# The first three projection units get their own order and one norm for all tokens

## The chip, the cores and the metric

The kernel runs on one core of a Trainium2 chip. The metric is the device time of one execution in microseconds (us), less is better. Where one profiled execution is read, times are from its first instruction.

## The reference

One step of a two-layer streaming encoder over 1056 tokens (1024 new frames and 32 frames of a running stream), model width 1024, all in float32. What the change touches is the entrance of layer 0:

```python
def _rmsnorm(x, g):
    xf = x.astype(jnp.float32)
    y = xf * lax.rsqrt(jnp.mean(xf * xf, axis=-1, keepdims=True) + EPS)
    return (y * g.astype(jnp.float32)).astype(x.dtype)

def _mixer_a(h, ctx, w_in, conv_w, w_out):
    gb, gc, u = jnp.split(h @ w_in, 3, axis=-1)
    z, new_ctx = _causal_dwconv(gc * u, ctx, conv_w)
    return (gb * z) @ w_out, new_ctx
```

`h` is `_rmsnorm(x, a_norm)`. Behind it come a gated feed-forward net with a width-3 convolution, a combined key/value projection, forgetting attention over 16 heads, and a second feed-forward net. The outputs are the normed stream, the new keys, values and forget logits, and the convolutions' last rows.

## The kernel before

Everything is held transposed: a tile is 128 features by 1056 tokens, and `x` is eight such tiles (`NK` = 8). A float32 product is made of three matmuls in a rounded format: each operand is split into a high part (ScalarE, `AF.Copy` into float32r) and a low part (VectorE, the rest), and `chain` adds high*high, high*low and low*high into one PSUM bank for each of the eight feature blocks.

A *unit* (`unit`) is one weight tile of 1024 by 128 against all tokens: three chunks `CH` of 352 tokens, 8 blocks, 3 matmuls, so 72 matmuls. `w_in` has 24 units. The mixer (`mixer`, its `make(t)`) takes them in threes: `gc` (unit `NK+t`), `u` (`2*NK+t`), then `gb` (`t`); gc times u, a convolution, times gb. The first three units here are gc, u and gb of t = 0, the fourth to sixth those of t = 1.

The row norm is applied after the product: it is one factor per token. `normed` splits each x tile (with the gain folded in), squares it on ScalarE and adds the squares (`square_add`: GpSimd, for the last tile VectorE) into `acc`. While the factor is not known, the first two units run with the blocks outermost (`outer`), as x tiles come in, and are evicted raw. Then `settle` calls `rstd`, chunk by chunk: four matmuls sum the squares of 4 x 88 tokens over the features (L334), ScalarE takes the square root, VectorE the reciprocal with a correction step, a diagonal tile `dg` is built, and one matmul with ones spreads the factor over all 128 rows (L348). `settle` multiplies the raw gc and u; units from the third on multiply on eviction (L294).

The loads stand on SP's queue in program order: gains, x0's first third, the first unit's weights in two pieces (blocks 0 to 1, then 2 to 7), the rest of x. The weight staging tile `wraw` has one buffer, so a unit's weights are asked for when the one before has been split; split weights (`wh`, `wl`) share four buffers. The order of the work on each engine is set by the tile framework's scheduler, which follows a timeline of its own, except inside `strict()`, where instructions of TensorE, VectorE and ScalarE keep their program order (all such instructions bear the line of the wrapper, L73). PSUM has eight banks' worth of tiles: three `d`, two double `s`, one `o`; `dbank` goes round d, d, d, s, s, o.

## Time and profile before

| | us |
|---|---|
| median of 3 runs | 2549.89 (2549.51 to 2549.95) |
| the profiled execution | 2550.09 |
| its span, first to last instruction | 2548.3 |
| mean granted TensorE clock | 0.989 |
| TensorE busy | 2471.9 (97%) |
| start of the fourth unit on TensorE | 64.67 |

In the rows of the profile PE is TensorE's matmuls, PEld its weight loads, DVE VectorE, ACT ScalarE, POOL GpSimd and SP the queue that issues the loads. A row names the line, the operation, output<-input and the shape; "xN" counts instructions merged into a row, whose duration is then that of all. A bracket holds the idle time before an instruction and what ended it. In tables by stretch the granted clock stands behind the engines' busy times, 1.00 being full speed.

### The profile page before, as it was taken

How to read it: one execution, taken by the hardware profiler on the slowest of the kernel's cores; microseconds unless marked ns; L12 is line 12 of the kernel's file. 1: busy time of each engine (PE TensorE's matmuls, PEld its weight loads, DVE VectorE, ACT ScalarE, POOL GpSimd, SP SyncE). 2: the span in 40 equal slices, each digit the busy share in tenths (PEclk: the TensorE clock that was granted, in tenths of full speed). 3: DMA queues.
4: the chain of work that ended last, by engine and by line, in shares of the span. 5: the costliest groups of instructions: out<-in, count | busy, mean ns of one | idle time of the engine just before them, and what ended most of it. 6: DMA issues, size and time to landing. Idle time of an engine off the chain costs nothing. (4 is left out here: it accounts for less than half of the span.)

```text
span 2548.3 us, 47227 instructions
## 1 busy us (share of the span) xinstructions
PE 2471.9 (97%) x18484; PEld 2433.1 (95%) x18484; DVE 1531.6 (60%) x2617; ACT 1216.5 (48%) x2388; POOL 899.3 (35%) x952
## 2 busy tenths in 40 slices
PE   7999999999999999998999999999999999999996
PEld 6999999999999999997999999999999999999996
DVE  5434438855555555665677677665875555555575
ACT  4111114555555555444566666653454555555454
POOL 3000012344444444342455444422244444443423
PEclk9999999999999999998999999999999999999998
DMA  3111123376766666631233222373247676666752
GB/s 111 45 48 50 42 77 98 70 120 120 122 119 114 116 118 119 139 113 50 75 80 80 77 76 71 80 251 104 72 88 125 116 121 119 111 117 116 122 141 69
DMA packets 147631, 254.76 MB, mean 100 GB/s; under 512 B 22352, under 2 KB 58320, under 8 KB 147408
## 3 DMA queue, kind: packets, MB, share of 16 engines
q0 software_dynamic: 41472, 77.88, 23.0%
q1 hardware_dynamic: 105936, 173.87, 22.7%
q8 instruction: 145, 2.38, 0.4%
q14 instruction: 78, 0.64, 0.1%
HBM read 130.52 MB, written 113.04 MB: 96 GB/s over the span
## 5 line engine op out<-in xcount | busy, mean ns | idle before, releaser
L711 PE MATMUL pb_p<-b,wb 128*128 128x264 f32 x6720 | 894.9, 284 | 1.8 <-ACT u L753 1.8
L711 PEld LDWEIGHTS pb_p<-b,wb 128*128 128x128 f32 x6720 | 850.0, 188 | 2.2 <-ACT u L753 2.2
L877 POOL DMA_DIRECT2D xd<-xs x288 | 262.1, 914 | 494.9 <-ACT xs L875 493.6
L875 ACT ACTIVATE xs<-pb_d 128x264 f32<-128x264 f32 x576 | 218.3, 387 | 349.4 <-PE pb_d L261 309.8
L259 PE MATMUL pb_d<-acth,wb 128*128 128x264 f32 x1152 | 327.8, 285 | 1.6 <-ACT xs L875 1.6
L260 PE MATMUL pb_d<-actl,wb 128*128 128x264 f32 x1152 | 327.5, 285 | 0.0
L261 PE MATMUL pb_d<-acth,wb 128*128 128x264 f32 x1152 | 327.3, 285 | 0.0
L259 PE MATMUL pb_d<-xh,wh 128*128 128x384 f32 (+2 forms) x864 | 285.3, 333 | 8.4 <-ACT xh L248 7.6
L260 PE MATMUL pb_d<-xl,wh 128*128 128x384 f32 (+2 forms) x864 | 285.2, 330 | 5.6 <-DVE xl L249 5.5
L261 PE MATMUL pb_d<-xh,wl 128*128 128x384 f32 (+2 forms) x864 | 283.6, 328 | 0.0
L478 DVE SCALAR_TENSOR_TENSOR y<-u,cv,y 128x1058 f32<-128x1058 f32 x186 | 238.8, 1329 | 54.9 <-ACT y L474 54.8
L259 PEld LDWEIGHTS pb_d<-acth,wb 128*128 128x128 f32 x1152 | 216.6, 188 | 2.8 <-ACT xs L875 2.5
L261 PEld LDWEIGHTS pb_d<-acth,wb 128*128 128x128 f32 x1152 | 216.8, 188 | 0.0
L260 PEld LDWEIGHTS pb_d<-actl,wb 128*128 128x128 f32 x1152 | 216.8, 188 | 0.0
L236 ACT ACTIVATE wh<-wraw 128x1024 fp32r<-128x1024 f32 (+1 forms) x69 | 72.3, 1047 | 259.6 <-PE pb_o L260 125.3
L460 POOL COPY u<-cv 128x4 f32<-128x4 f32 x96 | 63.5, 662 | 355.7 <-DVE u L668 256.9
L701 DVE TENSOR_TENSOR wb<-wr,wb 128x512 fp32r<-128x512 f32 x196 | 154.2, 788 | 56.0 <-ACT wb L700 44.7
L701 DVE TENSOR_TENSOR wb<-ws,wb 128x512 fp32r<-128x512 f32 x160 | 126.1, 789 | 98.6 <-ACT wb L700 98.6
L259 PEld LDWEIGHTS pb_d<-xh,wh 128*128 128x128 f32 x864 | 164.7, 191 | 9.8 <-ACT xh L248 8.0
L260 PEld LDWEIGHTS pb_d<-xl,wh 128*128 128x128 f32 x864 | 165.1, 191 | 7.9 <-DVE xl L249 7.4
L733 POOL TENSOR_TENSOR ws<-wr 128x512 f32<-128x512 f32 x80 | 121.7, 1521 | 134.9 <-DMA wr<-in_w_up 120.8
L261 PEld LDWEIGHTS pb_d<-xh,wl 128*128 128x128 f32 x864 | 164.8, 191 | 0.3
(347 smaller groups left out, 4964.2 us busy)
## 6 DMA issues: line engine op xcount, KB each, us to landing
xd<-xs POOLq DMA_DIRECT2D x288, 264.0 KB, 4.3
wr<-in_w_up SPq DMA_DIRECT2D x168, 256.0 KB
wr<-in_w_down SPq DMA_DIRECT2D x80, 256.0 KB
x<-xd SPq DMA_DIRECT2D x48, 264.0 KB
wraw<-in_w_in SPq DMA_DIRECT2D x23, 512.0 KB
xd<-x SPq DMA_DIRECT2D x64, 132.0 KB
wraw<-in_w_kq SPq DMA_DIRECT2D x16, 512.0 KB
xd<-x SPq DMA_DIRECT2D x16, 264.0 KB
```

The source lines that it names most:

```text
L236: nc.scalar.activation(h[:, i:j], raw[:, i:j], AF.Copy)
L259: nc.tensor.matmul(ps, wh, xh[:, c[0]:c[1]], start=(i == 0), stop=False)
L260: nc.tensor.matmul(ps, wh, xl[:, c[0]:c[1]], start=False, stop=False)
L261: nc.tensor.matmul(ps, wl, xh[:, c[0]:c[1]], start=False, stop=(i == n - 1))
L460: self.nc.gpsimd.tensor_copy(v, st.rearrange("p (a b) -> p a b", b=2))
L478: self.nc.vector.scalar_tensor_tensor(y, u[:, i:i + TC], w[:, i:i + 1], y, op0=OP.mult, op1=OP.add)
L701: nc.vector.tensor_sub(t[:, 1], src, t[:, 0].bitcast(F32))
L711: nc.tensor.matmul(ps[:, q, :QB], w[:, i, k], t[:, j, cs], start=(begin and k == 0 and n == 0), stop=(end and k == len(b) - 1 and n == 2), ...
L733: getattr(self.nc.gpsimd, "tensor_" + op)(dst, x, y)
L875: nc.scalar.activation(t[:, q * QB:(q + 1) * QB], ps, AF.Copy)
L877: nc.gpsimd.dma_start(d, t, accum_op=OP.add)
```

## The change

The first three units move into a function of their own, `opening`, which runs under `strict()`, so that its written order is the engines' order:

- Loads: each of the three weight tiles has its own staging slot, and the second unit's weights are asked for before x4, the third's after x7.
- High and low parts of all x tiles come first; the weights' blocks 2 to 7 of unit 1 are split after x1. The squares of x follow on ScalarE while unit 2 runs, and VectorE adds all of them. GpSimd does nothing here.
- A one-column square root at the start has ScalarE load the table with Sqrt before any other work.
- The third unit starts before the norm is known. Between its first and second chunk twelve matmuls sum the squares of all 1056 tokens; between its second and third three matmuls spread the factor. gc, u and gb are then all scaled by VectorE, chunk by chunk.
- Each product block runs chunk by chunk with its three matmuls together.

`mixer` takes the finished gc, u and gb for t = 0. From the fourth unit on, the order on each engine is the same as before, but for two matmuls of the attention that change places.

ScalarE at the start of the program, before and after (x_99 is x0, x_100 is x1 and so on; wr is the new staging slot, nrm the tile of the small norm steps):

```order
L236 ACTIVATE wh<-wraw 128x256
L236 ACTIVATE wh<-wraw 128x768
L248 ACTIVATE xh<-x_99,gain 128x352 x3
L307 ACTIVATE acc<-x_99 128x1056
L248 ACTIVATE xh<-x_100,gain 128x1056
L310 ACTIVATE sq<-x_100 128x1056
L248 ACTIVATE xh<-x_101,gain 128x1056
L310 ACTIVATE sq<-x_101 128x1056
```

```order
L73 ACT_TABLE_LOAD
L73 ACTIVATE nrm<-epst 88x1
L73 ACTIVATE wh<-wr 128x256
L73 ACTIVATE xh<-x_99,gain 128x352 x3
L73 ACTIVATE xh<-x_100,gain 128x1056
L73 ACTIVATE wh<-wr 128x768
L73 ACTIVATE xh<-x_101,gain 128x1056
```

The larger weight piece went behind x1, and the squares left the row of high parts; they stand behind the split of the second unit's weights now.

VectorE behind the last low part, before and after (x_106 is x7; the lines L237 are weight splits of later units):

```order
L249 SCALAR_TENSOR_TENSOR xl<-x_106,gain,xh 128x1056
L311 TENSOR_TENSOR acc<-acc,sq 128x1056
L237 TENSOR_TENSOR wl<-wraw,wh 128x1024 x2
L338 TENSOR_SCALAR nw<-pb_d 88x4
L339 RECIPROCAL nr<-ne 88x4
```

```order
L73 SCALAR_TENSOR_TENSOR xl<-x_106,gain,xh 128x1056
L73 TENSOR_TENSOR wl<-wr,wh 128x1024
L73 TENSOR_TENSOR sq<-sq 128x1056
L237 TENSOR_TENSOR wl<-wraw,wh 128x1024
L73 TENSOR_TENSOR sq<-sq 128x1056 x3
L73 TENSOR_TENSOR wl<-wr,wh 128x1024
L73 TENSOR_TENSOR sq<-sq 128x1056 x3
L237 TENSOR_TENSOR wl<-wraw,wh 128x1024
L73 TENSOR_SCALAR nrm<-pb_s 88x12
```

VectorE now does all seven adds and four weight splits between the last low part and the norm, and the norm's small steps come once, for 12 columns.

TensorE between the end of unit 2 and the third unit, before (a piece without gaps) and after (the rows of the norm alone, each standing behind 24 matmuls of the third unit's first and second chunk):

```order
L261 MATMUL pb_o<-xh,wl 128x352
L334 MATMUL pb_d<-ones,acc 88x1 x4
L348 MATMUL pb_d<-dg,ones 128x352
L334 MATMUL pb_d<-ones,acc 88x1 x4
L259 MATMUL pb_d<-xh,wh 128x352
```

```order
L73 MATMUL pb_d<-xh,wl 128x352
L73 MATMUL pb_s<-ones,sq 88x1 x12
L73 MATMUL pb_d<-xh,wh 128x352
...
L73 MATMUL pb_d<-xh,wl 128x352
L73 MATMUL pb_s<-dg,ones 128x352
L73 MATMUL pb_o<-dg,ones 128x352
```

The sums had stood between unit 2 and the third unit with nothing between them and the first broadcast; now a chunk of 24 matmuls stands ahead of each. The diff:

```diff
@@ -654,23 +654,146 @@
         self.nc.sync.dma_start(cw, taps)
         return st, cw, out
 
-    def mixer(self, x, parts, after):
+    def opening(self, x, gain):
+
+
+        nc, a = self.nc, self.a
+        ACT, DVE, PE = nc.scalar, nc.vector, nc.tensor
+        srcs = [a["w_in"][i].rearrange("p (k c) -> p k c", c=128) for i in (NK, 2 * NK, 0)]
+        raw = [self.slot("wr", [128, NK, 128]) for _ in srcs]
+        w = [[self.wp.tile([128, NK, 128], F32R, name=n, tag="w") for n in ("wh", "wl")] for _ in range(2)]
+        w.append([self.slot(n, [128, NK, 128], F32R) for n in ("wh", "wl")])
+        xs = [[self.keep("x" + i, dt=F32R) for i in "hl"] for _ in range(NK)]
+
+        def load(m, c=(0, TT)):
+            nc.sync.dma_start(x[m][:, slice(*c)], a["x"][m][:, slice(*c)])
+
+        def fetch(u, i=0, j=NK):
+            nc.sync.dma_start(raw[u][:, i:j], srcs[u][:, i:j])
+
+        def whigh(u, i=0, j=NK):
+            ACT.activation(w[u][0][:, i:j], raw[u][:, i:j], AF.Copy)
+
+        def wlow(u, i=0, j=NK):
+            DVE.tensor_sub(w[u][1][:, i:j], raw[u][:, i:j], w[u][0][:, i:j].bitcast(F32))
+
+        def high(m, c=(0, TT)):
+            ACT.activation(xs[m][0][:, slice(*c)], x[m][:, slice(*c)], AF.Copy, scale=self.gain[:, gain, m:m + 1])
+
+        def low(m, c=(0, TT)):
+            cs = slice(*c)
+            DVE.scalar_tensor_tensor(xs[m][1][:, cs], x[m][:, cs], self.gain[:, gain, m:m + 1],
+                                     xs[m][0][:, cs].bitcast(F32), op0=OP.mult, op1=OP.subtract)
+
+        def products(u, ks):
+            ws = [(w[u][0][:, k], w[u][1][:, k]) for k in range(NK)]
+            for t, c in zip(banks[u], CH):
+                self.chain(t, ws, xs, c, ks)
+
+        def evict(u, i):
+            for p, d in spread(CH[i], before[u]):
+                ACT.activation(out[u][:, d], banks[u][i][:, p.start - CH[i][0]:p.stop - CH[i][0]], AF.Copy)
+
+        load(0, CH[0])
+        fetch(0, 0, 2)
+        fetch(0, 2, NK)
+        for c in CH[1:]:
+            load(0, c)
+        for m in range(1, NK):
+            load(m)
+            if m in (3, 7):
+                fetch(m // 4 + 1)
+        before = (0, PAD, 0)
+        out = [self.slot("gc"), self.slot("u", [128, TC + PAD]), self.slot("gb")]
+        banks = [[self.dbank()[:, :c[1] - c[0]] for c in CH] for _ in range(2)]
+        warm = self.slot("nrm")[:SIDE, :3 * TT // SIDE].rearrange("p (i n) -> p i n", i=3)
+        e, v, r = (warm[:, i] for i in range(3))
+        ACT.activation(e[:, :1], self.epst[:SIDE], AF.Sqrt)
+        whigh(0, 0, 2)
+        high(0, CH[0])
+        wlow(0, 0, 2)
+        low(0, CH[0])
+        for c in CH[1:]:
+            high(0, c)
+            low(0, c)
+        products(0, range(1))
+        for m in range(1, NK):
+            high(m)
+            low(m)
+            if m == 1:
+                whigh(0, 2)
+                wlow(0, 2)
+            products(0, range(m, m + 1))
+        whigh(1)
+        wlow(1)
+        sq = [self.slot("sq") for _ in range(NK)]
+        for m in range(NK):
+            ACT.activation(sq[m], x[m], AF.Square)
+            if m:
+                DVE.tensor_add(sq[0], sq[0], sq[m])
+            products(1, range(m, m + 1))
+            if m == 1:
+                for i in range(3):
+                    evict(0, i)
+            if m == 4:
+                whigh(2)
+                wlow(2)
+        banks.append([self.dbank()[:, :c[1] - c[0]] for c in CH])
+        evict(1, 0)
+        ws = [(w[2][0][:, k], w[2][1][:, k]) for k in range(NK)]
+        self.chain(banks[2][0], ws, xs, CH[0])
+        n = TT // SIDE
+        ps = self.bank("s")[:SIDE, :n]
+        for i in range(n):
+            PE.matmul(ps[:, i:i + 1], sq[0][:, i * SIDE:(i + 1) * SIDE], self.ones[:, :1], start=True, stop=True)
+        ACT.activation(e, ps, AF.Sqrt, bias=self.epst[:SIDE], scale=1.0 / D)
+        DVE.tensor_scalar(v, ps, -0.5 / D, -0.5 * EPS, op0=OP.mult, op1=OP.add)
+        DVE.reciprocal(r, e)
+        DVE.tensor_mul(e, r, r)
+        DVE.tensor_mul(e, e, v)
+        DVE.scalar_tensor_tensor(r, e, 1.5, r, op0=OP.add, op1=OP.mult)
+        evict(1, 1)
+        evict(1, 2)
+        self.rs = self.slot("rstd")
+        dg = self.slot("dg")[:SIDE, :TT].rearrange("p (n c) -> p n c", c=SIDE)
+        self.chain(banks[2][1], ws, xs, CH[1])
+        for i, c in enumerate(CH):
+            b = slice(c[0] // SIDE, c[1] // SIDE)
+            shape = [SIDE, b.stop - b.start, SIDE]
+            DVE.tensor_mul(dg[:, b], self.ident[:SIDE, None, :SIDE].to_broadcast(shape),
+                           r[:, b, None].to_broadcast(shape))
+            ps = self.bank("sos"[i])[:, :c[1] - c[0]]
+            PE.matmul(ps, self.ones[:SIDE], dg[:, b].rearrange("p n c -> p (n c)"), start=True, stop=True)
+            ACT.activation(self.rs[:, slice(*c)], ps, AF.Copy)
+        for i, c in enumerate(CH):
+            if i == 2:
+                self.chain(banks[2][i], ws, xs, c)
+            for u in range(2):
+                for p, d in spread(c, before[u]):
+                    DVE.tensor_mul(out[u][:, d], out[u][:, d], self.rs[:, p])
+            DVE.tensor_mul(out[2][:, slice(*c)], banks[2][i], self.rs[:, slice(*c)])
+        return xs, out
+
+    def mixer(self, x, xs, opened, after):
         a, nc = self.a, self.nc
-        xs = [parts[k] for k in range(NK)]
         st, cw, out = self.convs(a["st_a"], a["cw_a"], NK)
 
         def make(t):
-            gc = self.slot("gc")
-            self.unit(a["w_in"][NK + t], xs, gc)
-            u = self.slot("u", [128, TC + PAD])
-            self.unit(a["w_in"][2 * NK + t], xs, u, PAD)
+            if t == 0:
+                gc, u, gb = opened
+            else:
+                gc = self.slot("gc")
+                self.unit(a["w_in"][NK + t], xs, gc)
+                u = self.slot("u", [128, TC + PAD])
+                self.unit(a["w_in"][2 * NK + t], xs, u, PAD)
             for p, d in spread((0, TT), PAD):
                 nc.vector.tensor_mul(u[:, d], u[:, d], gc[:, p])
             self.halo(u, st[:, t])
             self.tail(out[:, t], u)
             y = self.conv(u, cw[:, t])
-            gb = self.slot("gb")
-            self.unit(a["w_in"][t], xs, gb)
+            if t:
+                gb = self.slot("gb")
+                self.unit(a["w_in"][t], xs, gb)
             for p, d in spread((0, TT), PAD, PAD):
                 nc.vector.tensor_mul(y[:, d], y[:, d], gb[:, p])
             return self.split(y, "act", keep=False, cuts=spread((0, TT), PAD, PAD))
@@ -1351,19 +1474,11 @@
     nc = net.nc
     net.consts()
     x = [net.keep(f"x{m}") for m in range(NK)]
-    for m in range(NK):
-        for c in CH if m == 0 else ((0, TT),):
-            nc.sync.dma_start(x[m][:, c[0]:c[1]], a["x"][m][:, c[0]:c[1]])
-            if m == 0 and c == CH[0]:
-                net.ready.append(net.weights(a["w_in"][NK], cuts=((0, 2), (2, 8))))
-        if m == 1:
-            net.ready.append(net.weights(a["w_in"][2 * NK]))
     with net.phase(SLOTS):
-        f, acc, parts = net.normed(x, "x", 0, True)
-        for m in range(NK):
-            f(m)
-        net.start(acc, 2)
-        net.mixer(x, parts, net.normalise(x, 1))
+        net.fresh = 0
+        with net.strict():
+            opened = net.opening(x, 0)
+        net.mixer(x, *opened, net.normalise(x, 1))
     with net.phase(UPSLOTS, banks=UPBANKS):
         f, acc, parts = net.normed(x, "x", None)
```

## The prediction

> **What bounds the kernel now.** I read the page first, to see which engine sets the time.
>
> ```profile
> span 2548.3 us, 47227 instructions
> PE 2471.9 (97%) x18484; PEld 2433.1 (95%) x18484; DVE 1531.6 (60%) x2617; ACT 1216.5 (48%) x2388; POOL 899.3 (35%) x952
> ```
>
> TensorE is busy 97% of the span, so what the change can win is TensorE's idle and slow time in the stage it touches. The busy times by stretch, cut at the events of that stage, come second. Columns: stretch, length, busy time of PE, PEld, DVE, ACT, POOL with counts, granted clock, DMA share, GB/s.
>
> ```profile
> 7.64:13.00 5.36, 5.25 (x15) 4.17 (x16) 3.43 (x6) 5.30 (x7) 1.18 (x1) 1.00 0.99 398
> 13.00:23.50 10.50, 5.72 (x32) 4.84 (x31) 10.50 (x4) 10.50 (x11) 10.26 (x4) 1.00 0.45 177
> 43.70:46.37 2.67, 0.00 (x0) 0.03 (x1) 2.04 (x7) 1.10 (x2) 0.00 (x0) 0.52 0.25 57
> 48.78:53.90 5.12, 5.12 (x18) 5.12 (x19) 1.75 (x8) 0.26 (x1) 0.00 (x0) 0.50 0.01 2
> 53.90:64.67 10.77, 10.77 (x69) 10.30 (x69) 3.19 (x12) 1.19 (x3) 0.00 (x0) 0.99 0.01 2
> 64.67:76.21 11.54, 11.54 (x74) 11.54 (x73) 9.81 (x14) 3.43 (x4) 1.31 (x2) 1.00 0.16 45
> 76.00:300.00 224.00, 224.00 (x1399) 224.00 (x1398) 92.69 (x135) 36.53 (x39) 9.15 (x14) 1.00 0.15 45
> ```
>
> The last two rows are the yardstick. From 64.67 us TensorE never rests for 235 us, and a unit of 72 matmuls takes 11.54 us (0.16 each). The three units before that end at 64.67 us although they hold 34.6 us of matmuls: 30 us are lost. So the question is one: when does the fourth unit start after the change? Whatever that start gains, 235 us of unbroken TensorE work behind it carry on.
>
> The timeline, by engine, shows who is waited for in the first two units (start, duration, instruction, what ended the idle time).
>
> ```profile
> 4.48 0.42 ACT L236 ACTIVATE wh<-wraw 128x256 fp32r<-128x256 f32 x1 [2.46 <-DMA wraw<-in_w_in]
> 6.27 0.84 ACT L236 ACTIVATE wh<-wraw 128x768 fp32r<-128x768 f32 x1 [1.37 <-DMA wraw<-in_w_in]
> 7.02 1.53 ACT L248 ACTIVATE xh<-x,gain 128x352 fp32r<-128x352 f32 x3
> 7.64 1.14 PE L259 MATMUL pb_d<-xh,wh 128*128 128x352 f32 x2 [7.64 <-ACT xh L248]
> 9.59 1.18 ACT L248 ACTIVATE xh<-x,gain 128x1056 fp32r<-128x1056 f32 x1
> 10.67 1.07 ACT L310 ACTIVATE sq<-x 128x1056 f32<-128x1056 f32 x1
> 10.80 1.32 DVE L249 SCALAR_TENSOR_TENSOR xl<-x,gain,xh 128x1056 fp32r<-128x1056 f32 x1 [1.21 <-ACT xh L248]
> 11.82 19.81 POOL L311 TENSOR_TENSOR acc<-acc,sq 128x1056 f32<-128x1056 f32 x6 [10.51 <-ACT sq L310]
> 12.63 0.49 PE L261 MATMUL pb_d<-xh,wl 128*128 128x352 f32 x1
> 12.84 9.60 DVE L249 SCALAR_TENSOR_TENSOR xl<-x,gain,xh 128x1056 fp32r<-128x1056 f32 x3 [0.72 <-ACT xh L248]
> 13.16 0.32 PE L261 MATMUL pb_d<-xh,wl 128*128 128x352 f32 x1
> 25.78 8.19 DVE L249 SCALAR_TENSOR_TENSOR xl<-x,gain,xh 128x1056 fp32r<-128x1056 f32 x3
> 33.89 1.25 DVE L311 TENSOR_TENSOR acc<-acc,sq 128x1056 f32<-128x1056 f32 x1
> ```
>
> A low part (xl) takes VectorE 1.32 us before GpSimd's first add of squares starts at 11.82, and 9.60/3 = 3.2 us while those adds run back to back (six in 19.81, 3.3 each). The add that VectorE does at 33.89, with GpSimd silent, is 1.25 again. So the two engines hold each other up, the last low part is done only at 25.78 + 8.19 = 33.97, and TensorE waits for one low part after the other. The list of waits up to 70 us (us in total, times, longest) says so too, and no engine in it waits for x from a transfer:
>
> ```profile
> PE pb_d L260 <- DVE xl L249: 5.5, 4, 1.7
> ```
>
> The rows at 12.63 and 13.16 are the same matmul at half and at full speed (0.49 and 0.32): the clock is full from about 13.1.
>
> The third reading is the norm, and where TensorE stands around it.
>
> ```profile
> 41.41 0.71 PE L334 MATMUL pb_d<-ones,acc 128*88 128x1 f32 x8
> 42.19 1.06 ACT L236 ACTIVATE wh<-wraw 128x1024 fp32r<-128x1024 f32 x1
> 43.26 1.28 ACT L336 ACT_TABLE_LOAD   x1
> 43.28 1.23 DVE L237 TENSOR_TENSOR wl<-wraw,wh 128x1024 fp32r<-128x1024 f32 x1 [4.75 <-ACT wh L236]
> 45.70 0.52 DVE L344 TENSOR_TENSOR dg<-ident,nr 88x352 f32<-88x352 f32 x1
> 46.37 1.51 PE L348 MATMUL pb_d<-dg,ones 88*128 88x352 f32 x2 [4.25 <-DVE dg L344]
> 55.28 0.76 PE L348 MATMUL pb_s<-dg,ones 88*128 88x352 f32 x2
> 55.88 0.71 PE L334 MATMUL pb_s<-ones,acc 128*88 128x1 f32 x8
> 56.45 0.41 PE L260 MATMUL pb_d<-xl,wh 128*128 128x352 f32 x1
> 64.67 0.32 PE L259 MATMUL pb_s<-xh,wh 128*128 128x352 f32 x1
> ```
>
> After unit 2 TensorE sums the squares of the first 352 tokens and then stands for 4.25 us, through ScalarE's split of a weight tile, a table load (1.28 us), the square root and VectorE's chain up to the diagonal dg. In the idle stretch the granted clock falls to 0.50 and stays there until 53.9; in 48.78:53.90 only 18 matmuls run where 32 would.
>
> **The change part by part.** Times are from the start of the span; the forecast is the start of the fourth unit, now 64.67.
>
> *First matmul.* ScalarE now splits the first two weight blocks (0.42), then the first third of x0 (0.51, one of the three at 7.02), and only later the other six blocks. From 4.48 that is 5.5, with the wait for the smaller block and handovers 5.9, against 7.64. The two later thirds of x0 are seen by 7.5 at the latest (below), so TensorE stutters until x1.
>
> *The low parts.* GpSimd's six adds go, and ScalarE's eight squares move behind all eight high parts. What remains on ScalarE per x tile is 1.17 and on VectorE 1.25 from start to start, less than TensorE's 9 x 0.16 = 1.44. So the loads become the pace.
>
> ```profile
> 0.00:5.00 5.00, 0.00 (x0) 0.00 (x0) 0.49 (x5) 1.70 (x2) 0.70 (x6) 1.00 0.53 136
> 5.00:9.00 4.00, 1.35 (x3) 0.92 (x4) 2.21 (x4) 2.73 (x5) 0.00 (x0) 1.00 0.93 302
> 9.00:18.00 9.00, 6.89 (x28) 5.66 (x27) 7.07 (x5) 8.94 (x10) 6.02 (x3) 1.00 0.98 392
> 8.13 0.33 SPq L227 DMA_DIRECT2D wraw<-in_w_in  x1
> ```
>
> SP issues unit 2's weights before x4 now, where they waited for a free buffer until 8.13 and x7 stood behind them. Up to x7 the same 5.40 MB are asked for (gains 0.02, x 4.33, two units 1.05). The rows give 0.68 MB by 5 us, 1.89 by 9 and all of it by about 17.7. What lands is used about 1.1 us later (the 0.73 MB up to the six weight blocks are in at 5.15, ScalarE starts at 6.27). So x7 is seen at 18.8; high part 1.17, low part 1.32, handovers: 21.4; the last eight matmuls of unit 1 add 1.3: 22.7. VectorE's own chain ends no later: x1's low part from 10.5, seven of them at 1.25 and the six weight blocks at 0.9, 20.2.
> To this comes the slow start: matmuls are 5.12/18 = 0.28 apart at half speed, and so they run until 13.1 now, 5.4 us after the first. I let the clock be full at 15, after 3 us of unbroken work from x1's low part at 11.9; until then TensorE falls behind by some 4 matmuls that the loads don't hide, 0.6 us. **Unit 1 ends at 23.4.**
>
> *Unit 2*, 72 matmuls with all operands there (its weight split ends at 22.2 behind the last low part): 11.54, to **34.9**. Beside it lie the moved squares. ScalarE: 8 x 1.07, two weight splits of 1.06, three evictions of 0.41, in all 12 us from 19.9 with a wait for unit 1's end: done at 32.5. VectorE: seven adds at 1.25 and two weight splits at 1.22 follow them, done at 34.8. The sum of squares is wanted behind the third unit's first chunk at 38.8; the cover is 4 us, and each us beyond it would cost one. The eviction's row:
>
> ```profile
> 35.51 0.82 ACT L284 ACTIVATE gc<-pb_d 128x352 f32<-128x352 f32 x2 [10.57 <-PE pb_d L261]
> ```
>
> *Third unit and norm.* Its three chunks hold 11.54. The square sums of twelve blocks of 88 tokens now come together behind chunk 1: 0.57 for four (55.88 to 56.45), 1.7 for twelve. From the end of the table load to the first broadcast it takes 46.37 - 44.54 = 1.8 us now; two more dg at 0.5 make 2.8. The table load is gone from here, since Sqrt's set is loaded at the start, ahead of the first weights (ScalarE idles there until 4.48). Chunk 2 (3.85) covers the 2.8, and if it didn't, the rest would be a wait. The three broadcast matmuls take 0.60 each (55.28 to 55.88): 1.8. Chunk 3 covers rstd's evictions (3 x 0.41) and most of VectorE's scaling. The edit costs no TensorE work: three sums and broadcasts stood before too. **34.9 + 11.54 + 1.7 + 1.8 = 50.0.**
>
> The gain is 64.67 - 50.0 = 14.7 us: 1.8 from the earlier start, 4.7 in units 1 and 2 (33.8 us from first to last matmul now, 29.0 then), 8.2 in the third unit with its norm (23.3 now, 15.0 then).
>
> *What lies behind.* VectorE's scaling of gc, u and gb, nine pieces of 0.5, now stands in one row and partly behind chunk 3. Who waits for it: the fifth unit for gb's three banks, at 50.0 + 11.54 = 61.5. The last of them is scaled after u by gc (1.33), near 52: 9 us of cover. The sixth unit's banks are free when gc of the fourth is scaled:
>
> ```profile
> 64.56 1.33 DVE L668 TENSOR_TENSOR u<-u,gc 128x1024 f32<-128x1024 f32 x2
> 74.53 0.52 DVE L294 TENSOR_TENSOR gc<-pb_s,rstd 128x352 f32<-128x352 f32 x1
> ```
>
> That is 10 us after the fourth unit starts and was no wait (76.00:300.00 has none); it keeps that place. The fourth and fifth units' weight splits move up into units 2 and 3, where ScalarE and VectorE have room. I take nothing for all this.
>
> *Bounds.* If TensorE never waited after 5.9 and ran slow for 5 us, the start would be 5.9 + 34.6 + 3.5 + 2.3 = 46.3 (2531.7 us). If the loads are seen 1 us later and the clock is full only at 21, it is 53.3 (2538.7).
>
> **A rule weighed.** The rows show the clock full at 13.1 and again at 53.9, which are 5.4 and 7.5 us after the first matmul of the burst, so no fixed delay. The Trainium skill, "TensorE: Matmul & The Clock Gate", part 1, says that the clock is half by default and is raised only after a busy window of about 3.4 us, windows that run freely and not from the first matmul. By that rule the gaps before 11.9 may spoil a window, and the clock could come as late as two windows after 11.9, near 18.7. Both rows agree with free windows: 53.9 - 13.0 is twelve times 3.4. My sum stays with the rows; by the rule's worst case it would be the first rival's time.
>
> **The rivals.**
> 1. *The clock comes late.* TensorE's early work is broken by the waits for x0's later thirds, x1 and its low part. For it: 0.50 was granted through 5 us of unbroken matmuls (48.78:53.90). Against: 7.64:13.00 had gaps too and ended at full speed. Each us at half speed beyond 15 costs 0.45; full at 19 means start 51.8: 2537.3. Chance 0.11.
> 2. *Only the norm's gain comes.* The low parts stay late for some reason other than GpSimd, such as the loads: 6.5 us of the 14.7 fall away, 2541.9. Against: TensorE waited for xl, and no engine for x. Chance 0.06.
> 3. *Given back.* Some later wait sits on a load or a buffer rather than on TensorE, and the start moves without the end: 2550. Against: 235 us without a gap. The slot pool now holds eight squares and the weights at once, which could hold a later tile. Chance 0.04.
> 4. *Slower: VectorE can't carry the squares.* From 10.5 eighteen wide VectorE instructions (low parts, adds, weight splits) stand in a row ahead of the sums; each lasting d, they end at 10.5 + 18(d - 0.08), and 11.2 us of TensorE follow. At d = 1.32 the chunk hides them; the gain is gone at d = 2.5. If they kept the 3.5 that the xl rows show (because ScalarE or the loads slowed them, not GpSimd), the start would be 83: 2568 us. Against: 1.32 at 10.80, beside a ScalarE square and full loads; 1.25 at 33.89. Chance 0.03.
>
> **How the numbers follow.** The forecast has 0.76. The profiled execution took 2550.09 us, 0.20 above the median of the three runs (2549.89) and 1.8 above its own span; 2550.09 - 14.7 = 2535.4. The likeliest case alone spans 2532 (bound below) to 2537. With rival 1 added, to its upper bound of 2538.7, 0.87 is in; I give 2532 to 2540, the last us for a wait of VectorE on ScalarE's evictions. A measurement can tell about 0.2%, 5 us. Faster: 0.76 + 0.11 + 0.06 = 0.93; same 0.04; slower 0.03.
>
> **What would show it.** Right: GpSimd has no add before the mixer's end; x1 to x7's low parts take 1.3 us each and end near 21; unit 1's first eviction starts near 23.4; the twelve sums stand near 38.8 with no idle time before them; no granted clock of 0.5 after 19 in this stage; one table load before 60 us; the fourth unit (pb_s, the first L259 matmul) starts at 50; the 224 us after it are as before. Wrong: low parts above 2 us, a wait of TensorE before the sums or the broadcasts, a half clock beyond 19, or idle time in the fifth and sixth unit.

## The result and the profile after

The changed kernel takes 2536.63 us (median of five runs, 2535.95 to 2538.85) beside 2549.89 us for the kernel before on the same chip (2548.89 to 2551.27). The ratio is 0.9949, with a 95% interval of 0.9937 to 0.9962: faster by 13.3 us. The profiled execution took 2536.49 us. Its page gives the span and the busy times:

```profile
span 2534.7 us, 47216 instructions
PE 2469.2 (97%) x18484; PEld 2431.4 (96%) x18484; DVE 1520.3 (60%) x2613; ACT 1215.5 (48%) x2386; POOL 878.7 (35%) x946
```

The span is 13.6 us shorter with the same 18484 matmuls, and POOL has 946 instructions instead of 952: the six adds are gone. The stretches of the changed kernel, cut at its own events, show where the time left (columns as in the prediction's first table; the last row is everything from the fourth unit on):

```profile
5.13:13.00 7.87, 5.64 (x13) 3.69 (x14) 3.97 (x6) 4.60 (x6) 0.00 (x0) 1.00 1.00 358
13.00:16.40 3.40, 3.40 (x14) 3.40 (x13) 2.89 (x3) 2.15 (x3) 0.00 (x0) 1.00 1.03 420
16.40:24.08 7.68, 7.68 (x49) 7.68 (x48) 7.08 (x6) 6.73 (x8) 0.00 (x0) 1.00 0.52 198
24.08:35.60 11.52, 11.52 (x74) 11.52 (x73) 9.82 (x8) 8.75 (x11) 0.00 (x0) 1.00 0.15 47
35.60:50.72 15.12, 15.12 (x103) 14.48 (x102) 7.55 (x19) 3.48 (x8) 0.00 (x0) 1.00 0.12 36
62.07:286.00 223.93, 223.93 (x1398) 223.93 (x1397) 92.70 (x135) 36.27 (x39) 9.08 (x14) 1.00 0.16 45
50.94:2534.70 2483.76, 2425.63 (x18239) 2390.44 (x18238) 1487.88 (x2569) 1187.38 (x2349) 878.01 (x940) 0.99 0.47 100
```

The same last row of the kernel before, from its fourth unit on:

```profile
64.67:2548.30 2483.63, 2425.41 (x18240) 2390.29 (x18238) 1495.66 (x2572) 1188.07 (x2350) 879.17 (x940) 0.99 0.47 100
```

From 13.00 us TensorE is busy without a gap. The kernel before stood idle for 10.45 us between 13.00 and its fourth unit (6.2 ahead of the sums, 4.25 behind the first of them) and lost 3.8 us more to half speed. The fourth unit starts at 50.94 instead of 64.67, 13.73 us earlier, and what lies behind it takes 2483.76 us instead of 2483.63. So the whole gain was made before the fourth unit and nothing of it was given back. The timeline of the changed kernel, all engines, at the places that the prediction named:

```profile
5.13 0.66 PE L73 MATMUL pb_d<-xh,wh 128*128 128x352 f32 x1 [5.13 <-ACT xh L73]
15.83 5.26 DVE L73 SCALAR_TENSOR_TENSOR xl<-x,gain,xh 128x1056 fp32r<-128x1056 f32 x4 [0.51 <-ACT xh L73]
16.03 0.50 PE L73 MATMUL pb_d<-xh,wl 128*128 128x352 f32 x1
16.53 0.33 PE L73 MATMUL pb_d<-xl,wh 128*128 128x352 f32 x1
24.08 0.32 PE L73 MATMUL pb_s<-xh,wh 128*128 128x352 f32 x1
31.62 3.98 DVE L73 TENSOR_TENSOR sq<-sq 128x1056 f32<-128x1056 f32 x3
39.52 1.97 PE L73 MATMUL pb_s<-ones,sq 128*88 128x1 f32 x24
42.83 1.39 DVE L73 TENSOR_TENSOR dg<-ident,nrm 88x352 f32<-88x352 f32 x3
45.30 0.76 PE L73 MATMUL pb_s<-dg,ones 88*128 88x352 f32 x2
50.94 0.33 PE L259 MATMUL pb_s<-xh,wh 128*128 128x352 f32 x1
51.45 0.19 POOL L460 COPY u<-cv 128x4 f32<-128x4 f32 x1 [50.14 <-DVE u L790]
```

The last four low parts take 5.26/4 = 1.3 us each and end at 21.09. The clock becomes full between 16.03 and 16.53 (a matmul of the same shape falls from 0.50 to 0.33). The profile counts each float32 matmul of the norm as two instructions, so the twelve sums are "x24". VectorE's last adds end at 35.60, nearly 4 us before the sums that want them; the diagonals dg are done at 44.2, a good us before the broadcasts. Neither the sums nor the broadcasts show an idle time in front. GpSimd's first instruction after the program's start-up is at 51.45.

### The profile page after: what moved, and what is told of

Its sections match the earlier page's. It is cut to its first block, busy times and chain, and to the rows that moved or that the text cites. A ratio compares the mean times of both kernels' runs of the same rounds, so it can differ in the third digit from the quotient of the medians.

```text
span 2534.7 us, 47216 instructions
## 1 busy us (share of the span) xinstructions
PE 2469.2 (97%) x18484; PEld 2431.4 (96%) x18484; DVE 1520.3 (60%) x2613; ACT 1215.5 (48%) x2386; POOL 878.7 (35%) x946
## 5 line engine op out<-in xcount | busy, mean ns | idle before, releaser
L259 PE MATMUL pb_d<-xh,wh 128*128 128x384 f32 (+2 forms) x816 | 269.9, 331 | 0.8 <-DVE x L509 0.7
L260 PE MATMUL pb_d<-xl,wh 128*128 128x384 f32 (+2 forms) x816 | 266.8, 327 | 0.0
L261 PE MATMUL pb_d<-xh,wl 128*128 128x384 f32 (+2 forms) x816 | 266.7, 327 | 0.0
L236 ACT ACTIVATE wh<-wraw 128x1024 fp32r<-128x1024 f32 x65 | 68.9, 1061 | 257.1 <-PE pb_o L260 125.4
L824 DVE TENSOR_TENSOR wb<-wr,wb 128x512 fp32r<-128x512 f32 x196 | 153.5, 785 | 54.8 <-ACT wb L823 44.2
L823 ACT ACTIVATE wb<-wr 128x512 fp32r<-128x512 f32 x196 | 123.4, 630 | 70.3 <-PE pb_p L834 58.2
L259 PEld LDWEIGHTS pb_d<-xh,wh 128*128 128x128 f32 x816 | 154.5, 189 | 2.0 <-issue 1.0
L260 PEld LDWEIGHTS pb_d<-xl,wh 128*128 128x128 f32 x816 | 154.6, 189 | 0.3
```

Of the source, the lines that this page charges most:

```text
L236: nc.scalar.activation(h[:, i:j], raw[:, i:j], AF.Copy)
L259: nc.tensor.matmul(ps, wh, xh[:, c[0]:c[1]], start=(i == 0), stop=False)
L260: nc.tensor.matmul(ps, wh, xl[:, c[0]:c[1]], start=False, stop=False)
L261: nc.tensor.matmul(ps, wl, xh[:, c[0]:c[1]], start=False, stop=(i == n - 1))
L823: nc.scalar.activation(t[:, 0], src, AF.Copy)
L824: nc.vector.tensor_sub(t[:, 1], src, t[:, 0].bitcast(F32))
```

## The experiments

One table for all of them. Times are from the start of the span. "x7 low" is the end of the last low part, "unit 4" the start of the fourth unit. b1 and e1 to e7 were run once; for a1, e8 and e9 the time is the median of five, the other columns are of the one that was profiled. The kernel before took 2548.8 to 2552.8 us beside them (2548.8 beside b1, e5 and e6, 2552.8 beside e1 to e4, a median of 2550.3 beside the others).

| kernel | us | x7 low | unit 2 starts | sums start | unit 4 | from unit 4 to the end |
|---|---|---|---|---|---|---|
| before (profiled run) | 2550.09 | 33.97 | interleaved | 41.41 | 64.67 | 2483.6 |
| changed (profiled run) | 2536.49 | 21.09 | 24.08 | 39.52 | 50.94 | 2483.8 |
| b1: before, adds on VectorE | 2545.11 | 26.3 | interleaved | 36.04 | 58.79 | 2484.5 |
| e1: GpSimd busy again | 2541.82 | 29.24 | 31.10 | 46.52 | 57.93 | 2482.1 |
| e2: squares among the high parts | 2538.48 | 24.9 | 26.37 | 42.03 | 53.45 | 2483.2 |
| e3: norm ahead of the third unit | 2544.15 | 21.4 | 24.89 | 36.54 | 55.61 | 2486.8 |
| e4: no early table load | 2536.37 | 21.1 | 24.81 | 40.23 | 51.64 | 2482.9 |
| e7: e3 and e4 | 2543.77 | 21.3 | 24.93 | 36.58 | 55.91 | 2486.1 |
| e5: all of unit 1's weights first | 2536.75 | 21.3 | 23.13 | 38.55 | 49.94 | 2485.1 |
| e6: idle matmuls for the clock | 2536.17 | 21.1 | 22.95 | 38.38 | 49.76 | 2484.6 |
| a1: the changed kernel again | 2536.78 | 21.3 | 25.06 | 40.50 | 51.91 | 2483.2 |
| e8: other order of loads | 2536.64 | 19.95 | 22.23 | 37.66 | 49.08 | 2487.9 |
| e9: e8 and idle matmuls | 2535.95 | 19.9 | 23.81 | 39.24 | 50.62 | 2483.6 |

The changed kernel itself started its fourth unit at 50.94 in one execution and at 51.91 in another (a1). So 1 us of difference from 50.94 says nothing by itself, and distances in that column could be 1 us other.

### Did the adds move, or GpSimd?

**e1** gives GpSimd six adds again, of x1 to itself into a spare tile that nobody reads, beside the low parts.

```diff
+        spare = self.slot("spare")
+        for _ in range(6):
+            nc.gpsimd.tensor_add(spare, x[1], x[1])
         for m in range(1, NK):
             high(m)
```

> The changed kernel with six GpSimd adds of x1 to itself that nobody reads, issued before x1's high part, so that they run beside the low parts of x1 to x6; the squares stay where they are. Theory (GpSimd's adds are what made the low parts slow): a low part beside them takes 3.2 to 3.5 us instead of 1.3, the adds last about 20 us from 9.5, x7's low part ends near 30 instead of 21, unit 1 ends near 32 instead of 24.1, the fourth unit starts near 59 instead of 50.9, about 8 us later in all. Rival (the loads or ScalarE's squares between the high parts made them slow): low parts stay at 1.3 and the fourth unit at 50.9.

VectorE's and GpSimd's rows in its timeline, and TensorE's start of the fourth unit:

```profile
9.42 16.25 POOL L722 TENSOR_TENSOR spare<-x 128x1056 f32<-128x1056 f32 x6 [8.11 <-DMA x<-in_x]
15.03 14.21 DVE L73 SCALAR_TENSOR_TENSOR xl<-x,gain,xh 128x1056 fp32r<-128x1056 f32 x6
57.93 0.33 PE L259 MATMUL pb_s<-xh,wh 128*128 128x352 f32 x1
```

Six low parts (x2 to x7) take 14.21 us instead of 7.9, and the fourth unit starts 7.0 us later though no result of GpSimd is used. That is the collision of the two engines alone. Two neighbours of each engine singly:

```profile
16.98 2.84 POOL L722 TENSOR_TENSOR spare<-x 128x1056 f32<-128x1056 f32 x1
17.95 3.00 DVE L73 SCALAR_TENSOR_TENSOR xl<-x,gain,xh 128x1056 fp32r<-128x1056 f32 x1
19.91 2.84 POOL L722 TENSOR_TENSOR spare<-x 128x1056 f32<-128x1056 f32 x1
20.86 3.00 DVE L73 SCALAR_TENSOR_TENSOR xl<-x,gain,xh 128x1056 fp32r<-128x1056 f32 x1
```

The two engines take turns. The first add ends at 19.82 and the low part 1.1 us later, at 20.95; the second add ends at 22.75, 1.8 us behind that low part, and the next low part at 23.86, again 1.1 later. The duration in a row holds the wait for the other engine: four of the six low parts take 3.0 us, and the last two, with the adds over at 25.67, 1.3 again. The rows of the kernel before show the same turns, with low parts of 3.5. The Trainium skill, "SBUF — State Buffer", section "SBUF: two separate sides", calls it an exclusive lock on a pair of ports that GpSimd shares with a VectorE instruction of two inputs: one of them holds it for its whole instruction, the other is blocked. These turns agree with it. VectorE's weight split of 768 columns, beside the adds, takes 2.70 (0.95 in the changed kernel). What an add takes alone no run here shows.

**b1** does the reverse: it is the kernel before, with only the six adds moved from GpSimd to VectorE.

```diff
-                self.square_add(x[m], acc, m)()
+                self.square_add(x[m], acc, m, first)()
```

> The kernel before with one part of the change alone: VectorE adds all the squares of x, GpSimd none; everything else as before. Theory (GpSimd's adds held up the low parts): low parts at 1.3 us, x7's low part ends near 27 instead of 34, units 1 and 2 end near 35.5 instead of 41.4, the norm's stall and its half clock stay, the fourth unit starts near 59 instead of 64.7, the time falls by about 5.5 us. Rival (VectorE only trades GpSimd's hold-up for the adds in its own row): units 1 and 2 end at 40 or later and the time stays within 1.5 us.

Its timeline, VectorE and TensorE:

```profile
23.77 2.55 DVE L249 SCALAR_TENSOR_TENSOR xl<-x,gain,xh 128x1056 fp32r<-128x1056 f32 x2
36.04 0.71 PE L334 MATMUL pb_d<-ones,acc 128*88 128x1 f32 x8
40.98 1.51 PE L348 MATMUL pb_d<-dg,ones 88*128 88x352 f32 x2 [4.23 <-DVE dg L344]
58.79 0.32 PE L259 MATMUL pb_s<-xh,wh 128*128 128x352 f32 x1
```

The last two low parts take 2.55/2 = 1.3 each. The sums start at 36.04 instead of 41.41 (5.4 earlier), the fourth unit 5.9 earlier, although VectorE now does more work. The stall behind the sums stays, 4.23 beside 4.25. In the changed kernel the second unit ends at 35.60, so of the 5.8 us that units 1 and 2 gained, this one edit of a line brings 5.4 by itself. Its time, 2545.11 from one run, is 3.7 us under the kernel before beside it and 4.8 under the median of 2549.89; 5.5 were expected.

**e2** puts the squares back between the high parts on ScalarE; the adds stay where they are.

```diff
+        sq = [self.slot("sq") for _ in range(NK)]
+        ACT.activation(sq[0], x[0], AF.Square)
         for m in range(1, NK):
             high(m)
+            ACT.activation(sq[m], x[m], AF.Square)
...
-        sq = [self.slot("sq") for _ in range(NK)]
         for m in range(NK):
-            ACT.activation(sq[m], x[m], AF.Square)
```

> The changed kernel with the eight squares back between the high parts on ScalarE, as before; VectorE still adds them after the low parts and GpSimd stays idle. Theory (moving the squares matters too, since ScalarE would need 2.1 us per x tile where TensorE needs 1.44): low parts stay at 1.3, x7's high part ends near 23.8 instead of 19.7, unit 1 ends near 26.5, the fourth unit starts near 53.4, 2.5 us later. Rival (GpSimd alone was the brake): fourth unit at 50.9.

VectorE's and TensorE's timeline:

```profile
17.49 1.32 DVE L73 SCALAR_TENSOR_TENSOR xl<-x,gain,xh 128x1056 fp32r<-128x1056 f32 x1 [0.72 <-ACT xh L73]
24.99 0.43 PE L73 MATMUL pb_d<-xl,wh 128*128 128x352 f32 x1 [0.33 <-DVE xl L73]
53.45 0.32 PE L259 MATMUL pb_s<-xh,wh 128*128 128x352 f32 x1
```

The low parts keep their 1.32, but VectorE waits 0.72 us for each high part and TensorE for each low part; the fourth unit starts 2.5 us later than in the changed kernel's profiled run (1.5 later than in a1). So the squares' place counts too, in the changed kernel's order, in which unit 1 must be done before unit 2 begins. In b1 the squares stood among the high parts and it cost little; there TensorE had matmuls of unit 2 to do while it waited, which is an argument and not a test.

### Where the norm's 8 us come from

**e3** puts the whole norm ahead of the third unit, where it stood before, but still once for all tokens.

```diff
-        self.chain(banks[2][0], ws, xs, CH[0])
         n = TT // SIDE
...
-        self.chain(banks[2][1], ws, xs, CH[1])
...
         for i, c in enumerate(CH):
-            if i == 2:
-                self.chain(banks[2][i], ws, xs, c)
+            self.chain(banks[2][i], ws, xs, c)
```

> The changed kernel with the whole norm (twelve sums, the steps, three broadcasts) ahead of the third unit's first chunk, so that nothing covers the steps; the table with Sqrt is still loaded at the start. Theory: TensorE stands for about 2 us between sums and first broadcast and the clock stays full, since the pause is short: fourth unit near 52.9, 2 us later; so the placement gives 2 of the 8.2 us that were put to the norm, the rest was the table load, ScalarE's weight split ahead of it and the half clock that the longer pause brought. Rival (the placement is nearly all): a half clock follows here too and the fourth unit starts at 55 or later.

TensorE's timeline, and the stretch behind the wait, in e3 and then in the kernel before:

```profile
36.54 2.01 PE L73 MATMUL pb_s<-ones,sq 128*88 128x1 f32 x24
40.56 0.83 PE L73 MATMUL pb_s<-dg,ones 88*128 88x352 f32 x2 [2.01 <-DVE dg L73]
55.61 0.33 PE L259 MATMUL pb_s<-xh,wh 128*128 128x352 f32 x1
```

```profile
40.56:45.15 4.59, 4.58 (x13) 3.53 (x14) 1.69 (x4) 1.39 (x3) 0.00 (x0) 0.63 0.21 83
46.37:53.90 7.53, 7.53 (x27) 6.97 (x28) 2.11 (x8) 0.72 (x2) 0.00 (x0) 0.50 0.13 51
```

TensorE waits 2.01 us for dg, and after it the granted clock is 0.63 over 4.59 us, with 13 matmuls in them. My theory had the clock stay full after so short a pause; the rival was right. From the sums to the fourth unit it takes 55.61 - 36.54 = 19.07. The matmuls of the third unit with sums and broadcasts are 11.54 + 1.7 + 1.8 = 15.04 at full speed. The changed kernel takes 50.94 - 35.60 = 15.34 = 15.04 + 0.3 of handovers. In e3 the wait is 2.01 and the low clock costs 4.59 x 0.37 = 1.7, so 19.07 = 15.04 + 2.01 + 1.7 + 0.3. The same sum for the kernel before is 64.67 - 41.41 = 23.26 = 15.04 + 4.25 + 3.8 + 0.2, with 7.53 x 0.50 = 3.8.

**e4** leaves the early square root out, so that Sqrt's table is loaded when the norm first wants it; **e7** does the same in e3's order.

```diff
-        ACT.activation(e[:, :1], self.epst[:SIDE], AF.Sqrt)
```

> The changed kernel without the one-column square root at the start, so that ScalarE loads the table with Sqrt behind the sums. Theory: the load of 1.3 us lies under the third unit's second chunk, with 1.1 us to spare before: the first broadcast waits at most 0.3 us and the fourth unit starts at 50.9 to 51.2. Rival (the table load is on the path): 52.2.

> The changed kernel with the norm ahead of the third unit and without the early square root, so that the steps and the table load lie open together. Theory: TensorE stands 3.3 us instead of 2.0 between sums and first broadcast (the load's 1.3 us come on top) and the half clock lasts longer than the 1.9 us it cost in the run without cover; the third unit with its norm, from unit 2's end to the fourth unit's start, takes 20.5 to 22 us, against 19.1 without cover, 15.3 in the changed kernel and 23.3 before. Rival (the load is hidden by the sums or by the square root's wait): 19.1.

ScalarE's timeline in e4:

```profile
37.50 1.28 ACT L73 ACT_TABLE_LOAD   x1
42.24 0.27 ACT L73 ACTIVATE nrm<-pb_s,epst 88x12 f32<-88x12 f32 x1 [3.46 <-PE pb_s L73]
```

The load is done at 38.78, and ScalarE then waits 3.46 us for the sums. From unit 2's start to the fourth unit e4 takes 51.64 - 24.81 = 26.83, the changed kernel 50.94 - 24.08 = 26.86: the early load is worth nothing where a chunk of matmuls stands before the sums. (The fourth unit's 51.64 lies outside the expected 50.9 to 51.2 because unit 2 began 0.7 later.) TensorE's rows in e7:

```profile
36.58 2.01 PE L73 MATMUL pb_s<-ones,sq 128*88 128x1 f32 x24
40.89 0.83 PE L73 MATMUL pb_s<-dg,ones 88*128 88x352 f32 x2 [2.30 <-DVE dg L73]
55.91 0.32 PE L259 MATMUL pb_s<-xh,wh 128*128 128x352 f32 x1
```

Without a chunk in front it costs 0.3 us (2.30 of waiting beside 2.01), not the 1.4 to 3 that I expected. ScalarE's rows of e7 say why:

```profile
36.54 1.06 ACT L236 ACTIVATE wh<-wraw 128x1024 fp32r<-128x1024 f32 x1 [0.34 <-PE pb_o L73]
37.62 1.28 ACT L73 ACT_TABLE_LOAD   x1
```

Weight split and load end at 38.90, while the twelve sums last until 38.59. In the kernel before, the same two ended at 44.54 and the sums at 42.12, because there the split began 0.8 us behind the sums' start and only four of them stood there: 2.4 of the 4.25 us of stall were this overhang, 1.8 the chain from the square root to dg. In e7 the overhang is 0.3: the row of sums is 1.3 us longer, and the split begins with the sums. So the norm's gain of 7.9 us has two about equal parts. 23.26 falls to 19.33 in e7, where one norm for all tokens and the written order make the wait 2.30 instead of 4.25 and the half clock behind it shorter; no run takes these two apart. From there it falls to 15.34 through the norm's place between the chunks, which takes away the rest of the wait and the half clock behind it.

### What the early start is worth

**e5** splits all eight weight blocks before x0, as the kernel before did.

```diff
         whigh(0, 0, 2)
+        whigh(0, 2)
         high(0, CH[0])
         wlow(0, 0, 2)
+        wlow(0, 2)
...
-            if m == 1:
-                whigh(0, 2)
-                wlow(0, 2)
```

> The changed kernel with all eight weight blocks of unit 1 split before x0, as before, so that TensorE's first matmul comes near 7.6 instead of 5.1. The prediction put 1.8 us of the gain to the earlier start. Theory now (x1's low part at 12.0 and the half clock set unit 1's end, not the start): no loss, the fourth unit at 50.9; if the later matmuls fill the stretch 9.5 to 13.0 enough for the clock to be raised near 13 as before, even 49.7. Rival (the start counts as the prediction had it): 52.5 or later.

TensorE's timeline:

```profile
8.13 0.66 PE L73 MATMUL pb_d<-xh,wh 128*128 128x352 f32 x1 [8.13 <-ACT xh L73]
12.52 0.33 PE L73 MATMUL pb_d<-xh,wl 128*128 128x352 f32 x1
49.94 0.33 PE L259 MATMUL pb_s<-xh,wh 128*128 128x352 f32 x1
```

The first matmul is 3.0 us later and the fourth unit is 1.0 us earlier. What early matmuls gain, TensorE loses again later, waiting for x. Begun later, they stand closer together, and in this run the clock was full by 12.5; whether the one brought the other a single run can't show.

**e6** keeps TensorE busy from the start with 17 matmuls of ones into a bank that is not yet used (9 ahead of the first weight block, 2 and 6 among x0's chunks).

```diff
+        idle = self.bank("o")[:, :128]
+        def keep_busy(n):
+            for _ in range(n):
+                PE.matmul(idle, self.ones, self.ones, start=True, stop=True)
+        keep_busy(9)
...
+            keep_busy((2, 0, 6)[i])
```

> The changed kernel with 17 matmuls of ones with ones that nobody reads: nine ahead of the first real one, from about 1.1 us, two and six in the early gaps. Theory (half speed until 16.4 set unit 1's end): the clock is full from about 6 and stays so, TensorE then waits for low parts, unit 1 ends near 22.6 instead of 24.1 and the fourth unit starts near 49.4, 1.5 us earlier. Rival (loads and low parts set it): no change, 50.9.

TensorE, a matmul at full speed and the start of the fourth unit:

```profile
8.35 0.32 PE L73 MATMUL pb_d<-xh,wl 128*128 128x352 f32 x1
49.76 0.33 PE L259 MATMUL pb_s<-xh,wh 128*128 128x352 f32 x1
```

The clock is full by 8.35 and stays so; unit 2 starts at 22.95 instead of 24.08 and the fourth unit 1.2 us earlier. So unit 1's half speed costs 1.1 us in the profiled run and 2.1 in a1 (25.06), and the rest of unit 1 is the pace of x: the last low part ends at 21.1 in both. With the clock out of the way, as in e5 and e6, a first matmul 3 us earlier moves unit 2's start by 0.2 us (23.13 and 22.95).

### Is there more to win, and can one see it?

**a1** is the changed kernel unedited, timed once more. **e8** orders the loads and splits anew, **e9** adds e6's idle matmuls to it. The edit of e8:

```diff
         for m in range(1, NK):
             load(m)
-            if m in (3, 7):
-                fetch(m // 4 + 1)
+            if m == 7:
+                fetch(1)
+                fetch(2)
...
+        whigh(0, 2)
+        wlow(0, 2)
         for m in range(1, NK):
-            high(m)
-            low(m)
-            if m == 1:
-                whigh(0, 2)
-                wlow(0, 2)
+            for c in CH if m == 1 else ((0, TT),):
+                high(m, c)
+                low(m, c)
```

> The changed kernel itself once more, timed beside the two that follow: 2536.6 us within 0.1%, with the fourth unit at 49.8 to 51.7, by when the clock is raised (between 12.5 and 18 in the runs so far, and unit 1's end moves with it).

> The changed kernel with three moves in its opening: the six weight blocks are split while ScalarE and VectorE wait for x1, x1 is split in three pieces, and unit 2's weights are asked for behind x7. Theory (half speed until about 16 paces unit 1, operands only after that): x1's first matmuls run from 10.6 instead of 12.0, unit 1 ends near 22.9 instead of 24.1, the fourth unit starts near 49.8, the time falls by 1 us, no more than the scatter. Rival (loads pace unit 1): the later weights bring x4 to x7 1.3 us earlier and the same comes out; if neither counts, 50.9.

> Those three moves together with the 17 matmuls of ones that raise the clock early. Theory: with both brakes off unit 1 ends near 21.3, the fourth unit starts near 48.1 and the time is 2.7 us under that of the changed kernel, near 2534. Rival (unit 2's weights, asked for last, now come too late): TensorE waits ahead of unit 2 and the fourth unit starts at 49 or later.

Ratios to the kernel before, five runs each: a1 0.9946 (0.9933 to 0.996), e8 0.9947 (0.9934 to 0.9959), e9 0.9943 (0.993 to 0.9955). None can be told from the changed kernel. In the profiled runs e8 starts its fourth unit at 49.08, before the 49.8 that was expected. The rows from the fourth unit on, first of a1, then of e8:

```profile
51.91:2535.10 2483.19, 2426.31 (x18240) 2389.97 (x18238) 1491.65 (x2569) 1188.21 (x2349) 879.89 (x940) 0.99 0.46 100
```

```profile
49.08:2537.00 2487.92, 2429.42 (x18240) 2393.75 (x18238) 1491.74 (x2569) 1187.98 (x2349) 879.13 (x940) 0.99 0.46 99
```

e8 does start the fourth unit 2.8 us before a1 does, and its profiled run then takes 4.7 us longer behind it, 3.1 of these with TensorE busy on the same 18240 matmuls, that is, at a lower clock: added up from the traces' clock records, the clock is half for 47.6 us behind the fourth unit in a1 and for 61.1 in e8. One stretch in which this is to be seen, of the changed kernel and of e8:

```profile
1080.00:1200.00 120.00, 105.82 (x608) 98.09 (x609) 71.75 (x150) 56.33 (x95) 44.85 (x27) 0.90 0.29 87
```

```profile
1080.00:1200.00 120.00, 106.78 (x594) 98.58 (x595) 70.20 (x148) 54.86 (x93) 45.04 (x27) 0.86 0.29 87
```

The granted clock is 0.86 instead of 0.90 there, with 14 matmuls fewer in 120 us. Over all the profiled runs the part behind the fourth unit takes 2482.1 to 2487.9 us although its code is the same. So a gain of 1 to 3 us in the opening drowns, and e8 is neither shown better nor worse. The half clock explains this pair, but not the whole scatter (e4 has 54.1 us of it and took 2482.9 behind its fourth unit), and why its length differs from run to run stays open.

e9 missed its expectation (fourth unit at 48.1, measured 50.62). The rival, late weights, isn't what happened, as TensorE has no wait between 13 and unit 2's start. The clock fell back:

```profile
6.70:8.12 1.42, 0.21 (x3) 0.02 (x2) 0.02 (x1) 0.64 (x2) 0.00 (x0) 0.88 0.86 292
8.12:14.60 6.48, 6.48 (x24) 6.15 (x25) 5.90 (x8) 6.08 (x8) 0.00 (x0) 0.50 1.00 407
```

It had been full by 6.1; around 1.2 us without work it fell, and it was half for 6.5 us of unbroken matmuls.

## Why the prediction was right, point by point

The forecast was 2535.4 us in a range of 2532 to 2540; the median is 2536.63 and the profiled execution 2536.49. The mechanism was the forecast one: the opening ends earlier (50.94, forecast 50.0) and all of it reaches the end of the span. That the total came within 1.2 us is in part luck: five executions of the same kernel spread over 2.9 us, and in a1 its opening ended 1 us later.

- **First matmul**: 5.13, forecast 5.9. But the 1.8 us that the gain's split gave to the earlier start were wrong: e5 takes the early start away and loses nothing. What the start seemed to bring belongs to the low parts and the squares (5.8 us at the end of unit 2, of which b1 has 5.4).
- **Low parts**: 1.3 us each, the last done at 21.09 against "near 21". e1 confirms the cause that the two rows of 3.2 and 1.32 us suggested.
- **End of unit 1**: 24.08, forecast 23.4. The sum there has two slips: 22.7 + 0.6 is 23.3, and at the rates of its rows the 5.40 MB are in by 18.0, not 17.7, which together would make 23.6. The loads came a little sooner than that: the high part of x7 starts at 18.56, forecast 18.8. The mis-sized term is the clock's moment: 15 was assumed, about 16.4 came. The price for it was right: 0.45 for each us makes 23.4 + 0.63 = 24.03; and a1, where matmuls ran at half speed until 18.2, should end at 24.84 by it and ended at 25.06. So the first rival, the late clock, is what happened in a small way here and more fully in a1 (fourth unit at 51.91, the rival's 51.8 for a clock full at 19), and the time stayed at 2536.8. The late clock is even the usual case: e3, e4 and e7 have the same order up to unit 2 (e4 and e7 without the early square root) and begin unit 2 at 24.81 to 24.93, near a1's 25.06. With e6's clock full from 8.35 on, unit 1 ends at 22.95 beside my 22.7 without the slow start: the estimate of the loads held too. This stretch of a1 shows the half speed:

```profile
12.26:18.20 5.94, 5.94 (x20) 5.94 (x21) 5.45 (x5) 4.56 (x5) 0.00 (x0) 1.00 1.03 420
```

Twenty matmuls in 5.94 us are 0.30 apart, half speed, under a granted clock that the column gives as 1.00; so at the start of the program the spacing must be read, not the column. The same kernel had full speed at 16.4 in one run and at 18.2 in another. The Trainium skill's "TensorE: Matmul & The Clock Gate", part 1, puts such differences down to activity windows that run freely and don't begin with the kernel. The traces agree: in all of them the half-clock stretches between the first raise and the last fall take 3.41, 6.83, 10.24 or 13.65 us, once to four times the same length. The kernel has a part in the moment all the same, as e6 with 8.35 shows. The rows deserved a wider term than the single "15" that I took from them.

- **Unit 2**: 11.52, forecast 11.54. The adds end at 35.60 where I had 34.8, with 4 us of cover, as forecast: VectorE carries the squares, and the slower rival fell with the low parts' 1.3.
- **Third unit and norm**: 15.34, forecast 15.04. The 0.3 are the changes from one kind of matmul to the other around sums and broadcasts: the twelve sums take 1.83 instead of 1.7, the rest is spread over the handovers. No wait stands before either, and no half clock after 16.4.
- **Behind the fourth unit**: forecast unchanged, measured 2483.76 beside 2483.63. The scaling in one row on VectorE, the moved weight splits and the later buffers cost nothing that can be seen. 62.07:286.00 is unbroken, as 76.00:300.00 was.

Two statements on the norm were too simple. The removed table load was given as a part of its gain; e4 shows it at zero here, e7 at 0.3 us in the other place. And the gain was told as cover alone; half of it is there in e7 already, which has one norm and the written order but no cover.

## What to carry to other kernels

Where VectorE's instructions of one shape have two durations in a trace, look at what GpSimd does in the slow ones: moving work to GpSimd, or leaving it there, can cost VectorE more than doing the work itself (six adds moved onto VectorE let the fourth unit start 5.9 us earlier by themselves). Where TensorE waits on a short chain of small steps, count the wait and what the half-speed matmuls behind it lose together, here 4.25 + 3.8 us, and put independent matmuls before the wait; a chunk of 3.85 us was enough for both. An earlier first matmul is worth nothing while a later operand sets the pace.

## What the hardware showed that was not expected

- Behind a pause of 2.01 us after two us of one-column sums (e3) the granted clock was 0.63 for 4.6 us, and behind 1.42 us nearly without work (e9) it was 0.50 for 6.5 us. In the changed kernel the sums alone, 1.83 us with matmuls right behind, brought none.
- Full speed came at 16.4 and at 18.2 us in two executions of one kernel, at 12.5 (e5) and 8.35 (e6) where the early matmuls stood closer. Between the first raise and the last fall, half clock came in multiples of 3.41 us.
- Beside back-to-back adds of GpSimd a low part took 3.0 us instead of 1.3 (e1) and a weight split of 768 columns 2.70 instead of 0.95; the two engines took strict turns.
- The part of the program that no kernel here changed took between 2482.1 and 2487.9 us in the profiled runs, more than the last edits to the opening could bring.
